# Transposing the inner activations of the feed-forward layers with VectorE blocks and a DRAM tile instead of TensorE

## The chip, the cores and the metric

One core of one Trainium2 chip runs the whole program. The metric is the device time of one execution in microseconds (us), the median of several executions.

## The reference, cut to what matters

Two layers, each a feed-forward layer, a mixer (attention, a state-space branch and a gating branch) and a second feed-forward layer, on 256 tokens of width 1024. The mixer is not touched by the change. The feed-forward layer is this:

```python
D_MODEL, SEQ, DEPTH, FFN_HIDDEN = 1024, 256, 2, 2816

def swiglu_ffn(x, w_gu, w_down):
    gate, up = jnp.split(x @ w_gu, 2, axis=-1)
    return (jax.nn.silu(gate) * up) @ w_down

def reference(...):
    h = x
    for i in range(DEPTH):
        f1 = swiglu_ffn(rms_norm(h, ffn1_pre_g[i]), ffn1_w_gu[i], ffn1_w_down[i])
        h = h + 0.5 * rms_norm(f1, ffn1_post_g[i])
        h = h + rms_norm(hybrid_mixer(...), mix_post_g[i])
        f2 = swiglu_ffn(rms_norm(h, ffn2_pre_g[i]), ffn2_w_gu[i], ffn2_w_down[i])
        h = h + 0.5 * rms_norm(f2, ffn2_post_g[i])
    return h
```

The product `silu(gate) * up` comes out with tokens on the partitions; the matmul with `w_down` needs it with the 2816 inner channels on the partitions. The step between the two, a transpose, is what is changed.

## The kernel before

**Tiling.** The 256 tokens are two tiles of 128 (t = 0, 1). Every weight matrix comes in blocks of 128 x 1024 float32 (512 KB); `load(i)` (L159) fetches block i into one of six `raw` tiles by a transfer issued from SyncE's queue. `split(i)` makes two float32r tiles of it, `whi` by a ScalarE cast (L179) and `wlo` by a VectorE subtraction (L180), in eleven buffers each, and then issues `load(i + 6)`. `unit` runs three matmuls for each 128 x 512 piece of a block and each token tile: high x high (L212), low x high (L213), high x low (L214). So a block feeds 4 matmuls of each of these lines, 12 in all.

**Feed-forward layer (`ffn`).** The 2816 inner channels are taken in six chunks, five of 512 and one of 256. For each chunk `gated` runs the gate and up matmuls into PSUM tiles `gu`, and `evac`, a task of its own, turns them into `silu` (ScalarE, L389) and `hh` (VectorE, L394). Then, in the kernel before, `evac` transposes `hh` on TensorE into a PSUM tile `htr`, 128 x 128 at a time (L401): eight transposes for a chunk of 512, four for the one of 256. ScalarE copies `htr` into `hTh` (L407) and VectorE subtracts to make `hTl` (L408). These two are the stationary operands of the down matmuls `dn`, which come after all six chunks, channel block by channel block.

**Order of the work.** The order of each engine is that in which the Python program emits its instructions (a manual schedule). After each unit of matmuls `pump` advances a nominal clock by 0.65 us for every three matmuls of 512 columns, steps every task whose waiting time has run out, and emits at most one split. A task's waiting times stand in the table `W`: `yield W["hh"]` in `evac` lets 5.2 us of this clock pass between `hh` and its transposes. The down matmuls call `finish(es[k // 4])` before they use a chunk, which steps that chunk's `evac` to its end if it is not there yet.

**SyncE's queue** issues its transfers in order, and each waits for what it needs before those behind it are issued. The weight loads are nearly all that is in it.

**Buffers.** `silu`, `hh` and other short-lived tiles of 128 x 512 share the six buffers of tag `b2`; `hTh` and `hTl` of a chunk of 512 are in `b4`. `htr` shares the three PSUM tiles of tag `tr` with the other transposes.

Of the kernel before, what the change touches and what calls it, by code (L numbers as in the profile page):

```python
# [9 lines left out]
F32 = mybir.dt.float32  # L10
# [3 lines left out]
ALU = mybir.AluOpType  # L14
AX = mybir.AxisListType

P = 128
L = 2
S = 256
NT = S // P  # L20
D = 1024
KD = D // P
FF = 2816
# [21 lines left out]
ACC, TR = 5, 3  # L45


W = {'gw': 6.5, 'tr': 0, 'parts': 0, 'sq': 1.3, 'lead': 3.9, 'sq2': 5.2, 'hh': 5.2, 'x0': 0.65, 'cv': 5.2, 'cs': 6.5, 'xs': 0, 'dt1': 2.6, 'dt2': 0, 'dt3': 5.2, 'cb': 2.6, 'w1': 1.3, 'w2': 5.2, 'ys': 3.9, 'qk': 3.9, 'vv': 0, 'qs': 0, 'ex': 0, 'p1': 10.4, 'p2': 0, 'p3': 3.9, 'ge': 0, 'ln': 10.4, 'sv': 0, 'yc': 9.1, 'mg': 3.9}


@with_exitstack
def trunk(ctx, tc, a):
    nc = tc.nc
    V, A, G, T = nc.vector, nc.scalar, nc.gpsimd, nc.tensor
# [2 lines left out]
    ring = ctx.enter_context(tc.tile_pool(name="ring", bufs=1))  # L57
    big = ctx.enter_context(tc.tile_pool(name="big", bufs=1))
    sm = ctx.enter_context(tc.tile_pool(name="sm", bufs=2))
    psum = ctx.enter_context(tc.tile_pool(name="psum", bufs=1, space=bass.MemoryType.PSUM))  # L60
    ctx.enter_context(tc.manual_schedule())

# [3 lines left out]
    def b2(name, shape=(P, 512), dt=F32):  # L66
        return big.tile(list(shape), dt, name=name, tag="b2", bufs=B2)
# [4 lines left out]
    def accs(name):  # L72

        slots = {}

        def dst(key, t):
            if (key, t) not in slots:
                slots[key, t] = acc(name)
            return slots[key, t]

        return slots, dst

    def tr(name):
        return psum.tile([P, 512], F32, name=name, tag="tr", bufs=TR)
# [8 lines left out]
    ident, tri, mask = (con[:, o:o + P] for o in (C_ID, C_TRI, C_MASK))  # L93
# [59 lines left out]
    raws, parts = {}, {}  # L153
# [38 lines left out]
    lead = [0]  # L192
# [56 lines left out]
    def chunk(key, kt=KD, n=512):  # L249
        per = 1024 // n  # L250
        return [[(b * per + j, j * n, n, key, b * per + j == 0, b * per + j == kt - 1) for j in range(per)]
                for b in range(kt // per)]


    def rsqrt(ss, name, scale, eps=EPS, coef=1.0):

        ss = list(ss)
        v = small(name + "v", 1)
        G.tensor_scalar(v, ss[0], scale / coef ** 2, eps / coef ** 2, op0=ALU.mult, op1=ALU.add)
        if len(ss) > 1:  # L260
            G.tensor_scalar(v, ss[1], scale / coef ** 2, v, op0=ALU.mult, op1=ALU.add)
        r = small(name, 1, bufs=4)
        G.tensor_tensor(r, v, nhalf, op=ALU.pow)
        return r

    def sumsq(src, name):
        ss = small(name, 1, bufs=4)
        junk = b2("junk", (P, src.shape[-1]), BF16)
        A.activation(junk, src, AF.Square, accum_out=ss)
        return ss  # L270

    def halves(ps, hi, lo):

        p3 = ps.rearrange("p (k t) -> p k t", k=4)
        A.copy(hi, p3)
        V.tensor_tensor(lo, p3, hi.bitcast(F32), op=ALU.subtract)

    def to_parts(src, hi, lo, gcol=None, scale=None, cut=((0, 4), (4, 8)), gap=W["parts"], made=None):

        for k0, k1 in cut:  # L280
            m = k1 - k0
            ps = tr("xtr")
            for k in range(k0, k1):
                T.transpose(ps[:, (k - k0) * P:(k - k0 + 1) * P], src[:, k * P:(k + 1) * P], ident)
            ps = ps[:, :m * P]
            if gcol is None:
                o_h, o_l = (x[:, k0:k1, :] for x in (hi, lo))
                p3 = ps.rearrange("p (k t) -> p k t", k=m)
                if scale is None:
                    A.copy(o_h, p3)  # L290
                    V.tensor_tensor(o_l, p3, o_h.bitcast(F32), op=ALU.subtract)
                else:
                    A.activation(o_h, p3, AF.Copy, scale=scale)
                    V.scalar_tensor_tensor(o_l, p3, scale, o_h.bitcast(F32), op0=ALU.mult, op1=ALU.subtract)
            else:
                o_h, o_l = (x[:, k0:k1, :] for x in (hi, lo))
                xg = b2("xg", (P, m, P))
                V.tensor_tensor(xg, ps.rearrange("p (k t) -> p k t", k=m),  # L298
                                gcol[:, k0:k1, None].to_broadcast([P, m, P]), op=ALU.mult)
                A.copy(o_h, xg)  # L300
                V.tensor_tensor(o_l, xg, o_h.bitcast(F32), op=ALU.subtract)  # L301
            if made is not None:
                made.update(range(k0, k1))
            yield gap

    class XT:
# [6 lines left out]
        def new(self, t):  # L313
            self.hi[t] = b4(f"{self.name}h{t}", (P, KD, P), F32R)
            self.lo[t] = b4(f"{self.name}l{t}", (P, KD, P), F32R)
            return self.hi[t], self.lo[t]
# [7 lines left out]
    def pre(t, x, r2, gcol, cut, made):  # L324

        yield from to_parts(h[t], *x.new(t), gcol=gcol, cut=cut, gap=2.0, made=made)
        yield W["sq"]
        r2[t] = rsqrt([sumsq(h[t], "s2")], "r2", 1.0 / D)

    class After:  # L330
# [13 lines left out]
        def run(self, t, grow, coef, x, r2, gcol, out):  # L344
# [25 lines left out]
            if out is None:  # L370
                yield W["lead"]
                yield from to_parts(h[t], *x.new(t), gcol=gcol)
            chains[0] -= 1
            if out is None:
                yield W["sq2"]
                r2[t] = rsqrt([sumsq(h[t], "s2")], "r2", 1.0 / D)


    def ffn(x, r2, nxt, head=HOLD):
        hT = {}  # L380
        es = {}

        def evac(c, w, gate, up):
            silu, hh = {}, {}
            for t in range(NT):
                while gate(t) is None:
                    yield 0
                silu[t] = b2("silu")
                A.activation(silu[t][:, :w], gate(t), AF.Silu, scale=r2[t])  # L389
            for t in range(NT):  # L390
                while up(t) is None:
                    yield 0
                hh[t] = b2("hh")
                V.scalar_tensor_tensor(hh[t][:, :w], up(t), r2[t], silu[t][:, :w], op0=ALU.mult, op1=ALU.mult)  # L394
            yield W["hh"]
            n = w // P
            pt = {}
            for t in range(NT):
                pt[t] = tr("htr")
                for j in range(n):  # L400
                    T.transpose(pt[t][:, j * P:(j + 1) * P], hh[t][:, j * P:(j + 1) * P], ident)  # L401
            new = b4 if n > 2 else b2
            hT[c] = (new("hTh", (P, NT, n, P), F32R), new("hTl", (P, NT, n, P), F32R))
            for t in range(NT):
                hi, lo = (z[:, t] for z in hT[c])
                p3 = pt[t][:, :w].rearrange("p (k t) -> p k t", k=n)
                A.copy(hi, p3)  # L407
                V.tensor_tensor(lo, p3, hi.bitcast(F32), op=ALU.subtract)  # L408

        def gated(c, w):  # L410
            slots, dst = accs("gu")
            full = set()

            def part(key, o):
                return lambda t: slots[key, t][:, o:o + w] if (key, t) in full else None

            halves_ = 2 if w == 512 else 1
            items = [b for key in range(halves_) for b in chunk(key)]
            es[c] = spawn(evac(c, w, part(0, 0), part(1, 0) if halves_ == 2 else part(0, w)))
            gemm(items, x.h, x.l, dst, head=head if c == 0 else 0, on_done=lambda key, t: full.add((key, t)))  # L420

        for c, w in enumerate(FCH):
            gated(c, w)
        items = [[(k, 512 * j, 512, j, k == 0, k == KF - 1) for j in range(2)] for k in range(KF)]

        def hx(i):
            def get(k, t):
                finish(es[k // 4])
                return hT[k // 4][i][:, t, k % 4, :]
            return get  # L430

        slots, dst = accs("dn")
        after = After(slots, nxt)
        gemm(items, hx(0), hx(1), dst, tail=HOLD, on_done=after, ends=nxt[-1] is not None)
        return after.tasks
# [14 lines left out]
    def spatial_weights(l):  # L450
        ws = b4("wsp", (P, 8, P))
        nc.sync.dma_start(ws, a["sgw"][l].rearrange("g j i -> j g i"))
        gb = row("sgu_ln_g", l), row("sgu_ln_b", l)
        yield W["gw"]
        V.tensor_tensor(ws, ws, tri[:, None, :].to_broadcast([P, 8, P]), op=ALU.mult)
# [579 lines left out]
    return v.reshape(lay, cols // n, k // (per * P), P, 1024)  # L1035


def _gated(w):
    parts = []
    c0 = 0  # L1040
    for n in FCH:
        halves = [w[:, :, half + c0:half + c0 + n] for half in (0, FF)]
        if 2 * n == 512:
            halves = [np.concatenate(halves, axis=2)]
        parts += [_chunks(m)[:, 0] for m in halves]
        c0 += n
    return np.ascontiguousarray(np.concatenate(parts, axis=1))
# [63 lines left out]
```

## Time and profile before

| | us |
|---|---|
| executions | 1506.69, 1508.36, 1509.73 |
| median | 1508.36 |
| the profiled execution, its own time | 1507.58 |
| span of its core, first to last instruction | 1505.8 |
| what lies around the span | 1.8 |

The profiled execution is 0.8 us below the median. The granted clock of TensorE is 0.997 of full speed over the span, its level of 2.4 GHz. In the profile PE is the matmuls of TensorE, PEld its weight loads, DVE is VectorE, ACT is ScalarE, POOL is GpSimd and SP is SyncE; a "q" behind the name means the queue of instructions that issue transfers. A matmul's duration there covers its way through the array, and the next one starts before it ends; the distance from start to start is the time that it takes of TensorE.

### The profile page before, as it was taken

How to read it: one execution, taken by the hardware profiler on the slowest of the kernel's cores; microseconds unless marked ns; L12 is line 12 of the kernel's file. 1: busy time of each engine (PE TensorE's matmuls, PEld its weight loads, DVE VectorE, ACT ScalarE, POOL GpSimd, SP SyncE). 2: the span in 40 equal slices, each digit the busy share in tenths (PEclk: the TensorE clock that was granted, in tenths of full speed). 3: DMA queues.
4: the chain of work that ended last, by engine and by line, in shares of the span. 5: the costliest groups of instructions: out<-in, count | busy, mean ns of one | idle time of the engine just before them, and what ended most of it. 6: DMA issues, size and time to landing. Idle time of an engine off the chain costs nothing.

```text
span 1505.8 us, 18575 instructions
## 1 busy us (share of the span) xinstructions
PE 1491.6 (99%) x7026; PEld 1236.4 (82%) x7026; DVE 932.2 (62%) x1112; ACT 783.2 (52%) x1079; POOL 55.8 (4%) x98
## 2 busy tenths in 40 slices
PE   9999999999999999999999999999999999999998
PEld 7888888878888888888888888888788888888886
DVE  6655477666566858555475554876665677675552
ACT  6544367655374537444364443866554644464441
POOL 0000020000000000000000000200000000000000
PEclk9999999999999999999999999999999999999999
DMA  8766646335556536666566664654364565476640
GB/s 292 269 191 196 185 169 193 116 124 182 159 179 212 180 138 224 205 182 201 153 225 185 184 205 140 210 168 141 116 190 142 195 197 168 153 254 192 183 154 28
DMA packets 77913, 270.27 MB, mean 179 GB/s; under 512 B 8960, under 2 KB 12160, under 8 KB 77824
## 3 DMA queue, kind: packets, MB, share of 16 engines
q1 hardware_dynamic: 77248, 268.76, 55.8%
q8 instruction: 55, 0.90, 0.2%
q10 hardware_dynamic: 576, 0.33, 0.1%
q14 instruction: 34, 0.28, 0.1%
HBM read 268.01 MB, written 1.05 MB: 179 GB/s over the span
## 4 chain that ended last, share of the span: by engine, by line
PE 94%; DVE 4%; ACT 1%; issue 1%; DMA 0%; POOL 0%; SPq 0%; DVEq 0%; ACTq 0%; POOLq 0%
PE gu L214 10%; PE gu L212 10%; PE gu L213 10%; PE dn L214 5%; PE dn L212 5%; PE dn L213 5%; PE br L214 3%; PE br L212 3%; PE br L213 3%; PE gate L212 2%; PE gate L214 2%; PE gate L213 2%; DVE wlo L180 2%; PE xbc L212 1%; PE xbc L213 1%; PE xbc L214 1%
## 5 line engine op out<-in xcount | busy, mean ns | idle before, releaser
L180 DVE TENSOR_TENSOR wlo<-raw,whi 128x1024 fp32r<-128x1024 f32 x495 | 601.5, 1234 | 385.8 <-ACT whi L179 384.6
L179 ACT CAST whi<-raw 128x1024 fp32r<-128x1024 f32 x495 | 513.5, 1051 | 406.0 <-PE gu L214 166.6
L212 PE MATMUL gu<-whi,xh 128*128 128x512 f32 x704 | 277.7, 394 | 1.8 <-ACT xh L300 1.4
L213 PE MATMUL gu<-wlo,xh 128*128 128x512 f32 x704 | 275.2, 391 | 0.0
L214 PE MATMUL gu<-whi,xl 128*128 128x512 f32 x704 | 274.8, 390 | 0.0
L212 PEld LDWEIGHTS gu<-whi,xh 128*128 128x128 f32 x704 | 132.6, 188 | 29.6 <-ACT xh L300 1.8
L214 PEld LDWEIGHTS gu<-whi,xl 128*128 128x128 f32 x704 | 132.6, 188 | 27.9 <-DVE xl L301 0.4
L213 PEld LDWEIGHTS gu<-wlo,xh 128*128 128x128 f32 x704 | 132.6, 188 | 27.7 <-DVE wlo L168 0.9
L212 PE MATMUL dn<-whi,hTh 128*128 128x512 f32 x352 | 137.9, 392 | 0.0
L214 PE MATMUL dn<-whi,hTl 128*128 128x512 f32 x352 | 137.1, 389 | 0.0
L213 PE MATMUL dn<-wlo,hTh 128*128 128x512 f32 x352 | 136.9, 389 | 0.0
L214 PEld LDWEIGHTS dn<-whi,hTl 128*128 128x128 f32 x352 | 66.1, 188 | 13.8
L212 PE MATMUL gate<-whi,xh 128*128 128x512 f32 x192 | 77.3, 403 | 0.0
L213 PEld LDWEIGHTS dn<-wlo,hTh 128*128 128x128 f32 x352 | 66.1, 188 | 13.4
L212 PEld LDWEIGHTS dn<-whi,hTh 128*128 128x128 f32 x352 | 66.1, 188 | 13.4
L214 PE MATMUL gate<-whi,xl 128*128 128x512 f32 x192 | 75.0, 390 | 0.0
L213 PE MATMUL gate<-wlo,xh 128*128 128x512 f32 x192 | 74.8, 390 | 0.0
L300 ACT CAST xh<-xg 128x512 fp32r<-128x512 f32 (+1 forms) x25 | 15.1, 603 | 62.0 <-DVE xg L298 62.0
L214 PEld LDWEIGHTS gate<-whi,xl 128*128 128x128 f32 x192 | 36.0, 188 | 7.8
L389 ACT ACTIVATE silu<-gu,r 128x512 f32<-128x512 f32 (+1 forms) x48 | 31.4, 654 | 19.9 <-PE gu L214 19.8
L213 PEld LDWEIGHTS gate<-wlo,xh 128*128 128x128 f32 x192 | 36.1, 188 | 6.6
L212 PEld LDWEIGHTS gate<-whi,xh 128*128 128x128 f32 x192 | 36.1, 188 | 6.5
(244 smaller groups left out, 2256.5 us busy)
## 6 DMA issues: line engine op xcount, KB each, us to landing
raw<-in_mix SPq DMA_DIRECT2D x232, 512.0 KB, 4.1
raw<-in_gu SPq DMA_DIRECT2D x175, 512.0 KB, 4.4
raw<-in_dn SPq DMA_DIRECT2D x88, 512.0 KB, 3.8
row_ffn_post_g<-in_ffn_post_g SPq DMA_DIRECT2D x4, 512.0 KB, 4.6
wsp<-in_sgw SPq DMA_DIRECT2D x2, 512.0 KB, 5.8
row_sgu_ln_g<-in_sgu_ln_g SPq DMA_DIRECT2D x2, 512.0 KB, 6.4
row_sgu_ln_b<-in_sgu_ln_b SPq DMA_DIRECT2D x2, 512.0 KB, 7.7
row_mix_post_g<-in_mix_post_g SPq DMA_DIRECT2D x2, 512.0 KB, 5.7
```

The lines of the kernel that those rows point to most:

```text
L179: A.copy(hi, w)
L180: V.tensor_tensor(lo, w, hi.bitcast(F32), op=ALU.subtract)
L212: T.matmul(o, xh(k, t), hi[:, off:off + n], start=first, stop=False)
L213: T.matmul(o, xh(k, t), lo[:, off:off + n], start=False, stop=False)
L214: T.matmul(o, xl(k, t), hi[:, off:off + n], start=False, stop=last)
L300: A.copy(o_h, xg)
L389: A.activation(silu[t][:, :w], gate(t), AF.Silu, scale=r2[t])
```

## The change

TensorE's transposes of `hh` go, and with them `htr`. In their place:

- `swap_out`, right behind `hh`: one VectorE transpose of the 128 x w tile, which transposes each 32 x 32 block in its place, into a tile `xt`, and one transfer (SyncE's queue) of `xt` to a tile in DRAM. Once for each token tile.
- after 6.5 us of the nominal clock `swap_in`: four transfers for each token tile (SyncE's queue) bring the DRAM tile back as `hr`. Each fills 32 partitions and reads runs of w/4 float32 (512 bytes for w = 512, 256 bytes for w = 256).
- after 6.5 us more `hTh` and `hTl` are made of `hr`, which is in SBUF, by the same two instructions as before; they read and write in pieces of 32 elements. Between the two token tiles 0.65 us pass.
- the columns of the gate and up weights are put in another order on the host (`_woven`), so that the blocks come out in the right places.

`silu`, `hh`, `xt` and `hr` share the six `b2` buffers. The DRAM tiles have eight buffers.

```diff
+    dram = ctx.enter_context(tc.tile_pool(name="dram", bufs=1, space=bass.MemoryType.DRAM))
...
+    def swap_out(src, w):
+        xt = b2("xt")
+        V.transpose(xt[:, :w], src[:, :w])
+        rd = dram.tile([P, w], F32, name=f"swap{w}", tag=f"swap{w}", bufs=8)
+        nc.sync.dma_start(rd, xt[:, :w])
+        return rd
+
+    def swap_in(dst, rd):
+
+        v = rd.rearrange("(a i) (c e) -> c i a e", a=4, c=4)
+        for c in range(4):
+            nc.sync.dma_start(dst[32 * c:32 * c + 32], v[c])
...
-            yield W["hh"]
             n = w // P
-            pt = {}
-            for t in range(NT):
-                pt[t] = tr("htr")
-                for j in range(n):
-                    T.transpose(pt[t][:, j * P:(j + 1) * P], hh[t][:, j * P:(j + 1) * P], ident)
+            rd = {t: swap_out(hh[t], w) for t in range(NT)}
+            yield W["out"]
+            hr = {}
+            for t in range(NT):
+                hr[t] = b2("hr")
+                swap_in(hr[t][:, :w].rearrange("p (a e) -> p a e", a=4), rd[t])
+            yield W["in"]
             new = b4 if n > 2 else b2
             hT[c] = (new("hTh", (P, NT, n, P), F32R), new("hTl", (P, NT, n, P), F32R))
             for t in range(NT):
-                hi, lo = (z[:, t] for z in hT[c])
-                p3 = pt[t][:, :w].rearrange("p (k t) -> p k t", k=n)
-                A.copy(hi, p3)
-                V.tensor_tensor(lo, p3, hi.bitcast(F32), op=ALU.subtract)
+                hi, lo = (z[:, t].rearrange("p k (a j) -> p a k j", a=4) for z in hT[c])
+                r4 = hr[t][:, :w].rearrange("p (a k j) -> p a k j", a=4, k=n)
+                A.copy(hi, r4)
+                V.tensor_tensor(lo, r4, hi.bitcast(F32), op=ALU.subtract)
+                yield 0.65
...
+def _woven(w, n):
+
+    v = w.reshape(*w.shape[:-1], -1, n // P, 4, 32)
+    return np.ascontiguousarray(v.swapaxes(-3, -2)).reshape(w.shape)
...
-        halves = [w[:, :, half + c0:half + c0 + n] for half in (0, FF)]
+        halves = [_woven(w[:, :, half + c0:half + c0 + n], n) for half in (0, FF)]
```

The table `W` gains `'out': 6.5, 'in': 6.5`.

## Rows read from the trace of the kernel before

**Rows 1.** The page: busy time of each engine with its share of the span, TensorE's granted clock in 40 slices, and the shares of the chain of work that ended last.

```profile
PE 1491.6 (99%) x7026; PEld 1236.4 (82%) x7026; DVE 932.2 (62%) x1112; ACT 783.2 (52%) x1079; POOL 55.8 (4%) x98
PEclk9999999999999999999999999999999999999999
PE 94%; DVE 4%; ACT 1%; issue 1%; DMA 0%; POOL 0%; SPq 0%; DVEq 0%; ACTq 0%; POOLq 0%
```

**Rows 2.** The waits of the whole span: who waited, for whom, us in total, times, the longest; then, of the view of the tile `raw`, all the waits of TensorE for a block that was made from it (us, times).

```profile
ACT whi L179 <- PE gu L214: 166.6, 117, 1.7
ACT whi L179 <- PE dn L214: 90.1, 55, 1.7
...
  PEld gu L212: 1.5, 2
  PEld gu L213: 1.4, 3
  PEld dtps L561: 0.7, 2
  PE gu L212: 0.3, 1
```

**Rows 3.** TensorE in order of time around the last eight transposes of a chunk of 512 and around the four of the chunk of 256 in the first layer. Columns: start, us from it to the end of the piece, engine, line, what it writes and reads, count.

```profile
131.64 0.39 PE L214 MATMUL gu<-whi,xl 128*128 128x512 f32 x1
131.87 1.03 PE L401 MATMUL htr<-con,hh 128*128 128x128 f32 x8
132.66 0.48 PE L212 MATMUL gu<-whi,xh 128*128 128x512 f32 x1
...
134.12 0.39 PE L212 MATMUL gu<-whi,xh 128*128 128x512 f32 x1
...
142.28 0.39 PE L212 MATMUL dn<-whi,hTh 128*128 128x512 f32 x1
...
143.41 0.39 PE L214 MATMUL dn<-whi,hTl 128*128 128x512 f32 x1
143.64 0.60 PE L401 MATMUL htr<-con,hh 128*128 128x128 f32 x4
144.00 0.48 PE L212 MATMUL dn<-whi,hTh 128*128 128x512 f32 x1
...
145.24 0.39 PE L214 MATMUL dn<-whi,hTl 128*128 128x512 f32 x1
```

**Rows 4.** The instructions that touch the tile `htr`: the transposes with the least, median and greatest duration in ns, and their busy time over the whole span by engine (PE, PEld, DVE, ACT), overlaps counted once.

```profile
L401 PE MATMUL htr<-con,hh x176: 270/272/273, 41.2 to 1446.0; 128*128 128x128 f32 x176
...
0.00:1505.80 1505.80, 23.07 (x176) 20.59 (x176) 28.76 (x48) 24.09 (x48) 1.00 0.56 179
```

**Rows 5.** The tile `wlo` from the start to five moments: busy time and count of the instructions on PE (the matmuls of L213 that read it), PEld, and DVE (the blocks made, the first of them in two halves).

```profile
0.00:40.00 40.00, 16.80 (x40) 7.95 (x41) 20.36 (x18) 1.00 0.85 299
0.00:109.00 109.00, 54.81 (x138) 26.23 (x138) 53.23 (x45) 1.00 0.76 252
0.00:594.00 594.00, 298.31 (x763) 144.11 (x763) 240.55 (x199) 1.00 0.57 185
0.00:780.00 780.00, 401.01 (x1026) 193.52 (x1026) 321.44 (x266) 1.00 0.58 187
0.00:1338.00 1338.00, 684.84 (x1754) 330.86 (x1755) 542.04 (x448) 1.00 0.57 182
```

**Rows 6.** Two stretches of one chunk of 512 each, in the first and second feed-forward layer: busy us of PE, PEld, DVE, ACT and POOL with the count of instructions, then TensorE's granted clock, the share of the transfer engines, GB/s.

```profile
109.00:131.60 22.60, 22.60 (x105) 18.84 (x104) 12.42 (x12) 10.72 (x13) 0.00 (x0) 1.00 0.66 185
599.00:621.60 22.60, 22.60 (x105) 18.83 (x104) 12.77 (x13) 10.98 (x13) 0.00 (x0) 1.00 0.75 243
```

**Rows 7.** Groups of VectorE and ScalarE instructions by shape: busy us, mean ns of one, idle time before them.

```profile
L842 DVE TENSOR_SCALAR gate<-gate,rs 128x512 f32<-128x512 f32 x8 | 3.5, 480 | 0.0
L859 DVE TENSOR_TENSOR merged<-merged,gate 128x512 f32<-128x512 f32 x16 | 11.1, 692 | 0.6
L811 DVE SCALAR_TENSOR_TENSOR vg<-vg,mv,row_sgu_ln_g 128x1024 f32<-128x1024 f32 x4 | 5.1, 1284 | 0.1
L408 DVE TENSOR_TENSOR hTl<-htr,hTh 128x512 fp32r<-128x512 f32 x40 | 25.8, 686 | 1.8
L407 ACT CAST hTh<-htr 128x512 fp32r<-128x512 f32 x40 | 21.5, 589 | 13.9 <-PE htr L401 13.9
L300 ACT CAST xh<-xg 128x512 fp32r<-128x512 f32 x23 | 14.3, 620 | 59.1 <-DVE xg L298 59.1
```

**Rows 8.** Transfers. A group by what it loads, with KB each and the median us from issue to landing; the load `wsp`, whose runs in DRAM are 512 bytes, with its time to landing (least, median, greatest); a weight load's time in SyncE's queue (ns) and its time to landing; and the transfer engines in the stretch from 590 to 600 us, in which the first chunk of the second feed-forward layer ends.

```profile
wsp<-in_sgw SPq DMA_DIRECT2D x2, 512.0 KB, 5.8
raw<-in_gu SPq DMA_DIRECT2D x175, 512.0 KB, 4.4
...
DMA to landing us min/median/max: 5.6/5.8/5.9
...
L159 SPq DMA_DIRECT2D raw<-in_gu x175: 327/328/772, 2.6 to 1393.4; - x175
...
DMA to landing us min/median/max: 3.3/4.2/9.1
...
DMA packets 1052, 3.83 MB, mean 383 GB/s; under 512 B 116, under 2 KB 116, under 8 KB 1052
```

More of the change, by code (lines that the diff above doesn't have):

```diff
@@ L45 @@
 ACC, TR = 5, 3
-W = {'gw': 6.5, 'tr': 0, 'parts': 0, 'sq': 1.3, 'lead': 3.9, 'sq2': 5.2, 'hh': 5.2, 'x0': 0.65, 'cv': 5.2, 'cs': 6.5, 'xs': 0, 'dt1': 2.6, 'dt2': 0, 'dt3': 5.2, 'cb': 2.6, 'w1': 1.3, 'w2': 5.2, 'ys': 3.9, 'qk': 3.9, 'vv': 0, 'qs': 0, 'ex': 0, 'p1': 10.4, 'p2': 0, 'p3': 3.9, 'ge': 0, 'ln': 10.4, 'sv': 0, 'yc': 9.1, 'mg': 3.9}
+W = {'gw': 6.5, 'tr': 0, 'parts': 0, 'sq': 1.3, 'lead': 3.9, 'sq2': 5.2, 'hh': 5.2, 'x0': 0.65, 'cv': 5.2, 'cs': 6.5, 'xs': 0, 'dt1': 2.6, 'dt2': 0, 'dt3': 5.2, 'cb': 2.6, 'w1': 1.3, 'w2': 5.2, 'ys': 3.9, 'qk': 3.9, 'vv': 0, 'qs': 0, 'ex': 0, 'p1': 10.4, 'p2': 0, 'p3': 3.9, 'ge': 0, 'ln': 10.4, 'sv': 0, 'yc': 9.1, 'mg': 3.9, 'out': 6.5, 'in': 6.5}
 @with_exitstack
```

## The prediction

> **What bounds the kernel now.** I read the page first: TensorE is busy for 99% of the span at a granted clock of nine tenths or more in every slice, and the chain that ended last runs 94% over PE, 4% over DVE [rows 1]. A busy PE need not be one without slack, since a matmul's row overlaps the next, so I looked next for waits. TensorE waits for a block of weights only eight times, 3.9 us in all, while ScalarE waits for TensorE in 172 places before it may write the next `whi`, 257 us in all [rows 2]: the eleven block buffers are full and the helpers are ahead. How far ahead is counted from the tile `wlo`: up to 109 us, 44 blocks were made and 138 / 4 = 34.5 used, so 9.5 blocks lie ready; at 594 us 198 - 190.8 = 7; at 780 us 265 - 256.5 = 8.5; at 1338 us 447 - 438.5 = 8.5; at 40 us, just ahead of the first transposes, 17 - 10.3 = 6.7 [rows 5]. Of TensorE's own pace the timeline tells: 36 starts from 134.12 to 142.28 us, 0.227 us each [rows 3]. A block of 12 matmuls is 2.72 us, and seven blocks are 19 us of cover. So here the end is set by what TensorE is given to do, and an instruction taken off it in this stage shortens the kernel by its time from start to start.
>
> **What is removed.** The row of a transpose says 0.272 us, and 176 of them would be 47.9 us; with overlaps counted once they cover 23.1 us [rows 4]. Neither is what they cost. From the last matmul ahead of eight transposes to the seventh start behind them pass 134.12 - 131.64 = 2.48 us, where seven starts take 7 x 0.227 = 1.59: eight transposes cost 0.89 us, 0.79 of it before the next matmul starts and 0.10 in the slower starts behind it. The four of the last chunk cost 145.24 - 143.41 - 6 x 0.227 = 0.47 us [rows 3]. There are 4 feed-forward layers with five groups of eight and one of four: 20 x 0.89 + 4 x 0.47 = 19.7 us. The lower bound counts only the gap before the next matmul, 20 x 0.79 + 4 x (144.00 - 143.41 - 0.227) = 17.3 us; the upper one is the 23.1 us covered. I take 19.7, as it is the distance of starts that the chain is made of.
>
> **What VectorE gets.** One transpose of 128 x 512 for each token tile; the trace has none. From below it is bounded by the cheapest one-source instruction of this shape, 0.48 us, from above by one of twice the width, 1.28 us; I take the 0.69 of an ordinary instruction of this shape [rows 7], as it also has one element in and one out for each lane and column. That adds 2 x 0.69 = 1.4 us to a chunk (1.0 to 2.6) in which VectorE works 12.4 to 12.8 of 22.6 us [rows 6]: about 14, at most 15.4, of the 21.7 us that are left of the chunk without the 0.89. Behind the transposes in VectorE's order stands the `wlo` of a block that TensorE needs seven to ten blocks later; 1.4 us against 19 of cover cost nothing. With the cover gone they would cost TensorE 20 x 1.4 + 4 x 0.7 = 31 us.
>
> The Trainium skill, "VectorE: DVE Perf Modes", section "The three transpose paths", gives 311 ns for a VectorE transpose of 128 x 128 in 16 bits; by that figure four in float32 would be an estimate of up to 1.2 us a tile, and no run here shows it yet. It lies inside the bounds above.
>
> **What moves from PSUM to SBUF.** The cast that makes `hTh` now reads SBUF: 620 instead of 589 ns for such a cast; the subtraction 692 instead of 686 [rows 7]. Both are off the path, 24 x 2 x 0.04 = 2 us in all. That they walk in runs of 32 elements no row prices; at twice their time a chunk has 2.6 us more on each engine, still under the idle 9.8 us of VectorE and 11.6 of ScalarE [rows 6].
>
> **What SyncE and the transfers get.** Per chunk two transfers out and eight in: 10 x 0.33 = 3.3 us of issuing beside the 8 x 0.33 of the weight loads [rows 8], in 22 us. The first `swap_out` waits for VectorE's transpose, the first `swap_in` for the landing in DRAM; behind them in the queue stand weight loads, six blocks (16 us) ahead of their split. The bytes are 1 MB a chunk; at the 383 GB/s that the transfer engines reached when they were full [rows 8] that is 2.7 us, on engines busy for 66 to 75% of such a chunk [rows 6], so 78 to 87% afterwards. That counts short runs like long ones; from the other side, a load of the same 512 KB with runs of 512 bytes, `wsp`, took 5.8 us to land against the 4.4 of a weight load [rows 8]. So the two `hr` land some 6 us after their issue, and `evac` asks for them 6.5 us of its clock later, 6.8 in time (0.227 x 3 for 0.65). If they are late, ScalarE stands still before `hTh` with the `whi` of later blocks behind it, and the cover pays. Nobody needs `hTh` soon: the last chunks' are asked for behind 32 units of the down matmuls, 32 x 6 x 0.227 = 44 us later. Cost: nothing; bound, one late landing of the longest kind (9.1 us [rows 8]) in each of 24 chunks, 24 x 2.3 = 55 us of ScalarE, which its idle 11 us a chunk absorb.
>
> The rule that speaks against this change stands in the Trainium skill, "DMA: Bandwidth & Descriptors", section "Rules for kernel authors": do not transpose in a transfer by a rearranged access pattern, it is 19 times slower than the hardware's own transposing transfer. Here only whole runs of 128 floats are moved about, and the row of `wsp`, a load with such runs, shows 1.3 times a weight load, not 19 times; the rule is weighed below as a rival.
>
> **The sum.** On TensorE -19.7 us; everything else is added beside it. The profiled execution: 1507.58 - 19.7 = 1487.9 us; it lies 0.8 below the median, so the median goes to 1508.4 - 19.7 = 1488.7.
>
> **The rivals.**
> - *Part is given back.* In the first chunk of a layer the blocks are still being caught up: around 594 us the transfer engines run at 383 GB/s, all they gave anywhere, with 7 blocks ready [rows 5, 8]. The new megabyte puts the loads back by 2.7 us and VectorE by 1.4 more; if that reached TensorE in the first chunk of each layer, 4 x 4.1 = 16 us at worst, about 8 on a middle course: 1497. Against it: 7 blocks are 19 us.
> - *No gain.* TensorE's pace is set by the supply of blocks, so the freed time turns into waiting: 1508. For it speaks only that VectorE is on 4% of the chain [rows 1]; against it the 3.9 us of waits and the seven to ten blocks ready [rows 2, 5].
> - *Slower: `hr` lands late.* ScalarE stands before `hTh`, all splits behind it. It decides from a landing at 6.8 + 11.6 = 18.4 us after issue on, in every chunk, plus what the cover of 19 us in six chunks gives (3.2): above 21.6 us a chunk loses. At 25 us: 24 x 3.4 = 82 us lost, 1570. The rows nearest to it say 5.8 and 9.1 [rows 8].
> - *Slower: strided reads at a 19th of the rate.* If the rows in DRAM read back 19 times as slowly as a weight load's 4.4 us for 512 KB, a chunk would need 84 us of transfers instead of its 22: about 20 x 62 + 4 x 31 = 1360 us more, near 2870. The page of that rule is named above; the `wsp` row is against it.
>
> **How the numbers follow.** Full gain 0.80 (its own range 1485.3 to 1491.1, from the bounds 23.1 and 17.3); part given back 0.10; no gain 0.04; late landing 0.04; strided reads 0.02. The range takes in the first and most of the second: 1485 to 1496. What a measurement of this kernel can tell from no change is about 0.2%, 3 us: faster 0.80 + 0.10 = 0.90, same 0.04, slower 0.06. The predicted time is that of the full gain, 1488.7.
>
> **What would show it.** In the profile of the changed kernel: no matmul of L401, 6850 instead of 7026 matmuls, PE's chain at the same 0.227 us from start to start through the whole of a chunk, which lasts 21.8 instead of 22.65 us; VectorE's transposes near 0.7 us, 48 of them; waits of PE for `whi` or `wlo` still a few us. It would be wrong if PE showed gaps within the gate and up matmuls (a given-back gain, then the waits name DVE or a transfer), if ScalarE's wait before `hTh` for the transfer of `hr` were over 10 us a chunk, or if the pace of matmuls itself got slower beside the new transfers.

## The result, and the profile after

The changed kernel takes 1487.53 us (median; 1486.74 to 1488.53) against 1508.37 of the kernel before: a ratio of 0.9863, 95% interval 0.9846 to 0.9880, or 20.8 us less. The prediction was 1488.7, 19.7 us less. The profiled executions differ by the same: spans of 1505.8 and 1486.2 us, 19.6 apart.

The page of the changed kernel, the lines that answer to [rows 1]; the lines of the program are moved, so that the matmuls L212 to L214 are now L213 to L215, and L179, L180 are L180, L181:

```profile
PE 1472.1 (99%) x6850; PEld 1218.8 (82%) x6850; DVE 955.2 (64%) x1160; ACT 782.6 (53%) x1079; POOL 55.6 (4%) x98
PE 94%; DVE 4%; ACT 1%; issue 1%; POOL 0%; DMA 0%; DVEq 0%; ACTq 0%; POOLq 0%
```

176 matmuls fewer, PE's busy time 19.5 us shorter, and the same chain. The first down matmul of the first layer in the kernel before, then the same place in the changed kernel:

```profile
136.84 0.39 PE L212 MATMUL dn<-whi,hTh 128*128 128x512 f32 x1
```

```profile
131.94 0.39 PE L215 MATMUL gu<-whi,xl 128*128 128x512 f32 x1
132.16 0.39 PE L213 MATMUL dn<-whi,hTh 128*128 128x512 f32 x1
```

The down part starts 4.7 us earlier. Five groups of eight transposes lay ahead of it, and 5 x 0.89 is 4.5. What came in their place, on VectorE and ScalarE (groups by shape: busy us, mean ns | idle before, and for whom), and the transfers of the way back (count, KB each, median us to landing):

```profile
L277 DVE STREAM_TRANSPOSE xt<-hh 128x512 f32<-128x512 f32 x40 | 25.9, 687 | 0.0
L425 DVE TENSOR_TENSOR hTl<-hr,hTh 128x512 fp32r<-128x512 f32 x40 | 27.4, 686 | 8.3 <-ACT hTh L424 8.2
L424 ACT CAST hTh<-hr 128x512 fp32r<-128x512 f32 x40 | 24.7, 617 | 13.1 <-DMA hr<-swap 12.6 <-issue 0.2
...
hr<-swap SPq DMA_DIRECT2D x160, 64.0 KB, 4.9
```

Two chunks of 512, as [rows 6] showed them before (busy us of PE, PEld, DVE, ACT, POOL; granted clock, share of the transfer engines, GB/s), and the waits that matter: ScalarE for `hr`, and SyncE's queue at the way back:

```profile
109.00:131.00 22.00, 22.00 (x98) 18.21 (x98) 13.66 (x15) 10.72 (x12) 0.00 (x0) 1.00 0.80 240
596.00:618.00 22.00, 22.00 (x98) 18.21 (x97) 14.20 (x15) 10.98 (x13) 0.00 (x0) 1.00 0.91 308
...
ACT hTh L424 <- DMA hr<-swap: 19.4, 12, 4.5
...
SPq L286 <- DMA raw<-in_gu: 28.3, 21, 2.4
...
140.78 7.47 SPq L286 DMA_DIRECT2D hr<-swap  x8
```

TensorE is without a gap in both. VectorE has 1.2 to 1.4 us more, the transfer engines are at 80 and 91%, and ScalarE stood before `hTh` in 12 of 48 cases, 4.5 us at the longest. The eight transfers of a chunk's way back are in SyncE's queue for 5 to 7.5 us (the row is the short chunk of the first layer), not for the 2.6 that eight times 0.33 make: by the profile some wait for transfers issued before them.

### The profile page after: what moved, and what is told of

It reads as the page before. It is cut to its first block, busy times and chain, and to the rows that moved or that the text cites. A ratio compares the mean times of both kernels' runs of the same rounds, so it can differ in the third digit from the quotient of the medians.

```text
span 1486.2 us, 18786 instructions
## 1 busy us (share of the span) xinstructions
PE 1472.1 (99%) x6850; PEld 1218.8 (82%) x6850; DVE 955.2 (64%) x1160; ACT 782.6 (53%) x1079; POOL 55.6 (4%) x98
## 4 chain that ended last, share of the span: by engine, by line
PE 94%; DVE 4%; ACT 1%; issue 1%; POOL 0%; DMA 0%; DVEq 0%; ACTq 0%; POOLq 0%
PE gu L213 11%; PE gu L215 11%; PE gu L214 11%; PE dn L213 5%; PE dn L215 5%; PE dn L214 5%; PE br L213 3%; PE br L215 3%; PE br L214 3%; PE gate L215 2%; PE gate L213 2%; PE gate L214 2%; DVE wlo L181 2%; PE xbc L215 1%; PE xbc L213 1%; PE xbc L214 1%
## 5 line engine op out<-in xcount | busy, mean ns | idle before, releaser
L181 DVE TENSOR_TENSOR wlo<-raw,whi 128x1024 fp32r<-128x1024 f32 x495 | 600.2, 1232 | 331.1 <-ACT whi L180 319.8
L180 ACT CAST whi<-raw 128x1024 fp32r<-128x1024 f32 x495 | 512.8, 1051 | 380.9 <-PE gu L215 131.8
L213 PE MATMUL gu<-whi,xh 128*128 128x512 f32 x704 | 276.0, 392 | 1.4 <-ACT xh L316 1.4
L214 PE MATMUL gu<-wlo,xh 128*128 128x512 f32 x704 | 274.9, 391 | 0.0
L215 PE MATMUL gu<-whi,xl 128*128 128x512 f32 x704 | 274.8, 390 | 0.0
L213 PEld LDWEIGHTS gu<-whi,xh 128*128 128x128 f32 x704 | 132.7, 188 | 29.8 <-ACT xh L316 1.8
L215 PEld LDWEIGHTS gu<-whi,xl 128*128 128x128 f32 x704 | 132.6, 188 | 28.0 <-DVE xl L317 0.4
L214 PEld LDWEIGHTS gu<-wlo,xh 128*128 128x128 f32 x704 | 132.5, 188 | 27.9 <-DVE wlo L169 0.9
L213 PE MATMUL dn<-whi,hTh 128*128 128x512 f32 x352 | 137.5, 391 | 0.0
L215 PE MATMUL dn<-whi,hTl 128*128 128x512 f32 x352 | 137.0, 389 | 0.0
L214 PE MATMUL dn<-wlo,hTh 128*128 128x512 f32 x352 | 136.9, 389 | 0.0
L215 PEld LDWEIGHTS dn<-whi,hTl 128*128 128x128 f32 x352 | 66.1, 188 | 13.8
L213 PE MATMUL gate<-whi,xh 128*128 128x512 f32 x192 | 77.3, 403 | 0.0
L214 PEld LDWEIGHTS dn<-wlo,hTh 128*128 128x128 f32 x352 | 66.1, 188 | 13.5
L213 PEld LDWEIGHTS dn<-whi,hTh 128*128 128x128 f32 x352 | 66.1, 188 | 13.4
L215 PE MATMUL gate<-whi,xl 128*128 128x512 f32 x192 | 75.0, 391 | 0.0
L214 PE MATMUL gate<-wlo,xh 128*128 128x512 f32 x192 | 74.8, 390 | 0.0
L215 PEld LDWEIGHTS gate<-whi,xl 128*128 128x128 f32 x192 | 36.0, 188 | 7.7
L405 ACT ACTIVATE silu<-gu,r 128x512 f32<-128x512 f32 (+1 forms) x48 | 31.3, 654 | 19.8 <-PE gu L215 16.2
L214 PEld LDWEIGHTS gate<-wlo,xh 128*128 128x128 f32 x192 | 36.2, 188 | 6.6
L213 PEld LDWEIGHTS gate<-whi,xh 128*128 128x128 f32 x192 | 36.1, 188 | 6.6
```

The costliest lines, as they stand in the source:

```text
L180: A.copy(hi, w)
L181: V.tensor_tensor(lo, w, hi.bitcast(F32), op=ALU.subtract)
L213: T.matmul(o, xh(k, t), hi[:, off:off + n], start=first, stop=False)
L214: T.matmul(o, xh(k, t), lo[:, off:off + n], start=False, stop=False)
L215: T.matmul(o, xl(k, t), hi[:, off:off + n], start=False, stop=last)
```

## The experiments

Each edit is to the changed kernel. Ratios are to the kernel before, run on the same chip, with their 95% interval.

**No transposition at all.**

```diff
-            rd = {t: swap_out(hh[t], w) for t in range(NT)}
-            yield W["out"]
...
-            yield W["in"]
+            yield W["hh"]
+            hr = hh
```

> Leaves the transposition of the inner activations out altogether: hTh and hTl are made straight from hh, so the down matmuls multiply other numbers of the same shapes. Neither TensorE's transposes nor VectorE's, and no transfer through DRAM. Theory (the gain is TensorE's time for the transposes, and all that was added lies beside it): the same time as the changed kernel, 1487.5 us, within 1.5. Rival (the added work costs something that the gain hides): clearly under the changed kernel, by 3 us or more.

Measured: 1487.04 us, 0.9860 (0.9847 to 0.9873). The changed kernel's 0.9863 is within this: VectorE's transposes and 23 MB of transfers there and back cost nothing that can be measured, and the intervals are some 2 us wide to either side.

**TensorE's transposes put back beside the new path.**

```diff
             rd = {t: swap_out(hh[t], w) for t in range(NT)}
-            yield W["out"]
+            yield W["hh"]
+            for t in range(NT):
+                pt = tr("htr")
+                for j in range(n):
+                    T.transpose(pt[:, j * P:(j + 1) * P], hh[t][:, j * P:(j + 1) * P], ident)
+            yield W["out"] - W["hh"]
```

> The changed kernel with TensorE's transposes of hh put back at their old place, 5.2 us of the nominal clock behind hh, into a PSUM tile that nobody reads; hTh and hTl still come by VectorE and DRAM. Theory: 1487.5 + 19.7 = 1507.2 us, level with the kernel before. Rival (part of the gain is of another source, as the later making of hTh or the freed PSUM tiles): 1503 or less. Rival (the added work costs something): 1511 or more.

Measured: 1506.93 us, 0.9998 (0.9989 to 1.0006), level with the kernel before. So the gain is the time of the 176 transposes on TensorE: 1506.9 - 1487.5 = 19.4 us by the medians, 20.4 by the two ratios. Any other part of it is too small for these intervals.

**No waiting times.**

```diff
-'out': 6.5, 'in': 6.5}
+'out': 0, 'in': 0}
```

> The changed kernel with both waiting times at nothing ('out': 0, 'in': 0): the way back from DRAM is asked for as soon as the way out is issued, and ScalarE's cast to hTh stands in its queue at once. Theory (the blocks made ahead are cover enough): ScalarE waits some 8 to 12 us for hr in each of the 24 chunks, about 250 us in all against 19 in the changed kernel, SyncE waits for the landing in DRAM with weight loads behind it, and the time stays at 1487.5 within 2. Rival (the waiting times are what hides the transfers): 24 x 10 us less what ScalarE has idle, from 1495 up to 1600.

Measured: 1515.98 us, 1.0053 (1.0041 to 1.0065). The theory fell: 28 us lost. ScalarE's wait was as expected, but not what it held up. The waits of this kernel, and then ScalarE, VectorE and TensorE in order of time at the end of the first layer's gate and up matmuls, with the granted clock behind the stop and later:

```profile
ACT hTh L424 <- DMA hr<-swap: 251.7, 37, 11.7
...
PE dn L213 <- DVE hh L410: 20.5, 4, 6.5
...
134.82 0.62 ACT L424 CAST hTh<-hr 128x512 fp32r<-128x512 f32 x1 [10.61 <-DMA hr<-swap]
...
139.09 0.83 ACT L405 ACTIVATE silu<-gu,r 128x256 f32<-128x256 f32 x2
...
140.55 0.87 DVE L410 SCALAR_TENSOR_TENSOR hh<-gu,r,silu 128x256 f32<-128x256 f32 x2
...
134.14 0.39 PE L215 MATMUL dn<-whi,hTl 128*128 128x512 f32 x1
141.08 0.80 PE L213 MATMUL dn<-whi,hTh 128*128 128x512 f32 x1 [6.55 <-DVE hh L410]
141.67 0.63 PE L214 MATMUL dn<-wlo,hTh 128*128 128x512 f32 x1
142.10 0.63 PE L215 MATMUL dn<-whi,hTl 128*128 128x512 f32 x1
...
141.00:146.00 5.00, 4.92 (x15) 3.98 (x16) 2.20 (x5) 0.00 (x0) 0.00 (x0) 0.67 0.95 301
146.00:150.00 4.00, 4.00 (x20) 3.30 (x19) 0.00 (x0) 0.00 (x0) 0.00 (x0) 1.00 0.73 252
```

ScalarE stands 10.6 us before the cast of the last full chunk. Behind it in its order is the `silu` of the short chunk, whose matmuls end 10.9 us after the full one's; VectorE's `hh` waits for that `silu`, and the down matmul at 141.08 takes the PSUM tile that this `hh` reads. TensorE waits there once in each of the four layers, 20.5 us in all, and behind this stop the granted clock is 0.67 for 5 us, that is, partly at the lower level. ScalarE's other waits, over 200 us, cost nothing, as the next run shows.

**The waiting times only where the short chunk follows.**

```diff
-            yield W["out"]
+            yield W["out"] if c == 4 else 0
...
-            yield W["in"]
+            yield W["in"] if c == 4 else 0
```

> Both waiting times at nothing, as in the run without lead, except in the chunk ahead of the short one (c = 4), which keeps 6.5 and 6.5. New theory (what a late hr holds up are not the splits but silu and hh of the next chunk, whose PSUM tiles TensorE needs; only the short chunk follows so soon that its silu stands behind the cast of hr): ScalarE still waits some 200 us for hr in all, TensorE has none of the four stops at the start of the down matmuls, 1487.5 us within 2. Old theory of the splits as what is held up: the wait is nearly as long as without lead, so about 1512.

Measured: 1487.93 us, 0.9871 (0.9857 to 0.9886). The whole gain is back, with ScalarE's wait for `hr` still at 213.5 us; of TensorE's waits the longest in all is again the mixer's:

```profile
ACT hTh L424 <- DMA hr<-swap: 213.5, 29, 14.0
...
PE ctr L513 <- DVE ssw L682: 3.1, 2, 1.6
```

Four places of 24 needed the waiting times.

**Short runs: weights not reordered, 128 bytes a run, sixteen transfers for a token tile.**

```diff
-        v = rd.rearrange("(a i) (c e) -> c i a e", a=4, c=4)
-        for c in range(4):
-            nc.sync.dma_start(dst[32 * c:32 * c + 32], v[c])
+        v = rd.rearrange("(a i) (k c j) -> c a i k j", a=4, c=4, j=32)
+        d = dst.rearrange("p a (k j) -> p a k j", j=32)
+        for c in range(4):
+            for b in range(4):
+                nc.sync.dma_start(d[32 * c:32 * c + 32, b], v[c, b])
```

> The changed kernel without the new order of the gate and up weights' columns: the way back reads runs of 32 floats (128 bytes) instead of 128 (512 bytes), in sixteen transfers for each token tile instead of four. Theory (bytes and packets count, and short runs are not much slower): 4 times the packets of the way back, about 3 us more of transfers a chunk and 24 more issues in SyncE's queue, 10 us a chunk; hr lands later, ScalarE waits more, the time stays at 1488 to 1492. Rival (short runs are ruinous): 84 us a chunk, over 2500 us; a rate of a quarter would give some 8 us more a chunk and still be covered.

Measured: 1713.13 us, 1.1363 (1.1349 to 1.1378). Neither number. A stretch as long as a chunk of before, and one of TensorE's waits:

```profile
109.00:131.00 22.00, 22.00 (x87) 17.94 (x87) 10.23 (x11) 6.45 (x8) 0.00 (x0) 0.88 0.55 167
...
PE dn L213 <- ACT whi L180: 29.0, 5, 8.3
```

The transfer engines are not full, at 55%. TensorE waits 136 us for `hh`, and here also 29 us for `whi`: the cover of blocks made ahead runs out in the down parts. To tell the count of transfers from the length of their runs, the next run has the count alone.

**Long runs, but sixteen transfers for a token tile.**

```diff
         for c in range(4):
-            nc.sync.dma_start(dst[32 * c:32 * c + 32], v[c])
+            for b in range(4):
+                nc.sync.dma_start(dst[32 * c:32 * c + 32, b], v[c, :, b])
```

> The changed kernel with its runs of 512 bytes, but in sixteen transfers for each token tile instead of four, as many as in the run with short runs. Theory A (the count of transfers is the cost: SyncE issues them one by one at 0.4 to 0.6 us and weight loads stand behind them): near the 1713 us of the short runs, 1650 or more. Theory B (short runs are the cost, in the issue or in the engines): 1488 to 1510.

Measured: 1602.27 us, 1.0637 (1.0615 to 1.0658), between the two theories. The count alone costs 115 us, the short runs on top 111. The issue in SyncE's queue with its ns (least, median, greatest), with short runs; with long runs the way back of one chunk in that queue, ScalarE at the same time, and two waits of TensorE's weight loads:

```profile
L288 SPq DMA_DIRECT2D hr<-swap x768: 538/597/1718, 46.7 to 1682.3; - x192
```

```profile
132.06 16.16 SPq L287 DMA_DIRECT2D hr<-swap  x32
...
142.22 0.62 ACT L425 CAST hTh<-hr 128x512 fp32r<-128x512 f32 x1 [9.73 <-DMA hr<-swap]
...
149.51 0.62 ACT L425 CAST hTh<-hr 128x512 fp32r<-128x512 f32 x1 [5.72 <-DMA hr<-swap]
...
PEld dn L213 <- DVE hh L411: 41.9, 8, 6.9
PEld gu L213 <- DVE hh L411: 40.3, 9, 6.4
```

32 transfers are 16.2 us of SyncE's queue with long runs (a median of 0.42 each, the rest waits) and at 0.60 each 19 us with short ones, of a chunk of 21.8 that also needs its weight loads issued. The second `hr` lands some 17 us after the first issue, ScalarE stands before `hTh` twice, 15 us in this chunk, and `silu` and `hh` are late in ordinary chunks too. The profiled executions are 112 us apart: 78 of it is more idle time of PE (91.8 us against 14.1), the other 34 is more busy time for the same matmuls (1506.6 against 1472.1), at a mean granted clock of 0.974.

**Each VectorE transpose nine times.**

```diff
-        V.transpose(xt[:, :w], src[:, :w])
+        for _ in range(9):
+            V.transpose(xt[:, :w], src[:, :w])
```

> The changed kernel with each VectorE transpose made nine times: 16 more of 0.67 us in a chunk of 512, 10.8 us on VectorE, which then has 24.4 us of work in a chunk of 21.8. Theory of the splits as cover: 2.6 us too much in each of five chunks and less in the short one, 13 to 15 us a layer against 19 us of cover, so 1488 to 1492. Theory of silu and hh: hr comes 10.8 us later and hh of the short chunk stands behind the transposes, TensorE stops at the start of the down matmuls in each layer, 4 times 5 to 10 us: 1510 to 1530.

Measured: 1664.39 us, 1.1041 (1.1021 to 1.1060), over both numbers, on the side of `silu` and `hh`. Two of TensorE's waits, one of ScalarE's, and the two `silu` of one chunk:

```profile
PE dn L213 <- DVE hh L411: 89.7, 8, 15.8
...
PE gu L213 <- DVE hh L411: 49.1, 9, 7.4
...
ACT silu L406 <- DVE xt L278: 89.9, 20, 5.7
...
78.76 0.69 ACT L406 ACTIVATE silu<-gu,r 128x512 f32<-128x512 f32 x1 [5.25 <-DVE xt L278]
80.80 0.69 ACT L406 ACTIVATE silu<-gu,r 128x512 f32<-128x512 f32 x1 [1.35 <-DMA swap<-xt]
```

139 us are for `hh`, in the full chunks too; I had counted stops at the short one alone. `silu` was late in its turn by a thing I had not thought of: the `b2` buffer that it is to write is one that the transposes of the chunk before still use. The first `silu` starts when the nine transposes of one token tile are through, the second has to wait for the transfer of an `xt` on top. None of the longer waits is for a block of weights. The rest is slower matmuls: the mean granted clock was 0.952, and PE's busy time for the same matmuls grew by 33 us, from 1472.1 to 1505.5.

**Twice the bytes.**

```diff
+        for r in range(2):
+            more = dram.tile([P, w], F32, name=f"more{w}", tag=f"more{w}", bufs=16)
+            nc.sync.dma_start(more, xt[:, :w])
         return rd
```

> The changed kernel with two more transfers of every xt to DRAM tiles that nobody reads: 1 MB more a chunk of 512, which doubles the bytes of the new path, and four more issues in SyncE's queue. Theory (while the transfers fit in a chunk and hr comes before the silu of the short chunk is held up, they cost nothing): 2.7 us more on transfer engines that are busy for 80 to 91% of a chunk, just full; hr lands some 3 to 5 us later, ScalarE's wait for it goes from 19 to 50 or 100 us, 1488 to 1492. Rival (no room left): stops of TensorE at the start of the down matmuls, 1495 or more.

Measured: 1486.67 us, 0.9857 (0.9842 to 0.9872). Two chunks, the waits for `hr` in all (us, times), and the longest of a full chunk:

```profile
109.00:131.00 22.00, 22.00 (x99) 18.22 (x98) 14.40 (x17) 10.61 (x13) 0.00 (x0) 1.00 0.92 307
596.00:618.00 22.00, 22.00 (x99) 18.22 (x98) 13.48 (x15) 10.77 (x13) 0.00 (x0) 1.00 0.95 322
...
  DMA hr<-swap: 103.4, 26
...
79.00 0.62 ACT L427 CAST hTh<-hr 128x512 fp32r<-128x512 f32 x1 [7.95 <-DMA hr<-swap]
```

Engines at 92 and 95%, 103 us of waits on ScalarE, 4 us each and up to 8 in a full chunk, and no loss: the changed kernel has room for this.

**The transfers alone transpose, 4 bytes a run.**

```diff
-        V.transpose(xt[:, :w], src[:, :w])
...
+            for k in range(n):
+                nc.sync.dma_start(d[:, k, :], rd[:, k * P:(k + 1) * P].rearrange("t p -> p t"))
```

> The transfers alone make the transposition: hh goes to DRAM as it is, and the way back reads one float32 at a time, 65536 runs of 4 bytes for a token tile; no VectorE transpose, and no new order of the weights' columns. It is the case of the rival of strided reads. If a chunk then needs 84 us for its way back, 22 chunks' worth cost 22 x 84 us of transfers beside the weight loads: about 2700 to 3000 us. If runs that short cost no more than the 512-byte ones (the rule does not hold here): 1490 to 1700.

Measured: 3544.88 us (one execution). This is above both ranges. The issue of the way back in SyncE's queue:

```profile
L287 SPq DMA_DIRECT2D hr<-swap x176: 377/13484/15932, 45.8 to 3495.5; - x176
```

Eight of them make a chunk of 512: 8 x 13.5 = 108 us, where I had guessed 84. So the rival of the strided reads was a real one for runs of one element, and none for runs of 128. The 108 us are 25 times the 4.4 in which a weight load of as many bytes lands [rows 8]. The Trainium skill, "DMA: Bandwidth & Descriptors", section "Rules for kernel authors", puts such a transfer at 19 times the hardware's transposing one. No run here has that one, so its ratio is neither shown nor refuted; that the pattern is ruinous is.

**The same for q and k in the mixer.** The transposes of q and k (64) made by VectorE and DRAM as well, k landing in the operand itself, q with one ScalarE copy; the weights' columns of both are reordered.

```diff
+            rd = [swap_out(toks[t], 512) for t in range(NT)]
+            yield W["out"]
+            for t in range(NT):
+                swap_in(o[:, t].rearrange("p a k j -> p a (k j)"), rd[t])
...
-            yield from transposed(toks, lambda t: o[:, :, t * P:(t + 1) * P], "a")
```

> The changed kernel, with the transposes of q and k in the mixer made in the same way: 64 of TensorE's transposes less, 16 VectorE transposes and 160 transfers more; k lands from DRAM straight in the operand of the score matmuls, without a ScalarE copy, q is copied once by ScalarE. Theory: 8 groups of eight at 0.89 us, 7.1 us less, and up to 3 us more as TensorE's waits at the old transposes go (two of 1.6 us behind ssw): 1477.5 to 1480.4. Rival (the queues of the mixer have no room, or k is late): 1487 or more.

Measured: 1491.51 us, 0.9896 (0.9882 to 0.9911): 4 us slower than the changed kernel. TensorE's waits in the changed kernel, and in this one, with VectorE at the place, and the stretch of the branch with the lowest granted clock in each:

```profile
PE ctr L513 <- DVE ssw L682: 3.2, 2, 1.6
PE seg L680 <- DVE xg L314: 1.6, 2, 0.8
...
312.00:318.00 6.00, 6.00 (x21) 4.78 (x20) 4.26 (x5) 3.78 (x9) 0.00 (x0) 0.72 0.28 85
```

```profile
PE yd L711 <- DVE ssw L688: 5.9, 3, 2.7
PE seg L680 <- DVE xg L314: 3.2, 2, 1.6
PE yd L711 <- DVE xs L671: 2.9, 2, 1.5
...
307.10 1.29 DVE L277 STREAM_TRANSPOSE xt<-qtok 128x512 f32<-128x512 f32 x2
308.32 0.65 DVE L314 TENSOR_TENSOR xg<-xtr,par 128x512 f32<-128x512 f32 x1
...
318.00:330.00 12.00, 9.34 (x34) 7.17 (x34) 8.80 (x12) 5.70 (x12) 0.00 (x0) 0.72 0.47 129
```

Here TensorE waits for VectorE's state-space branch, in order. The waits grow from 4.8 to 12.0 us, as much as the 7.1 us of transposes, and the stretch with a clock of 0.72 is 12 us long instead of 6. So PE's busy time falls by only 3.4 us (1472.1 to 1468.7), while its idle time grows by 7.8. For the wait for `xg` the rows show VectorE's transposes right ahead of it; that they also make `ssw` and `xs` late was not shown by itself.

**Later emission of the branch.**

```diff
-'w2': 5.2,
+'w2': 7.8,
```

> The kernel with q and k transposed by VectorE and DRAM as well, and the waiting time w2 of the state-space branch raised from 5.2 to 7.8 us, so that TensorE's instructions that wait for ssw come later in its order. Theory (the 7.1 us of transposes went into TensorE's waits for ssw, as VectorE's transposes stand ahead of ssw): these waits shrink from some 15 us to under 6, 1478 to 1484. Rival (the branch itself is then late, and what follows waits for it): 1490 or more.

This is the version with q and k and a longer `w2`. Measured: 1505.31 us, 0.9983 (0.9974 to 0.9993). The rival was right. The wait for `ssw` that the edit was aimed at shrank from 5.9 to 3.9 us, but the branch's end, which nothing covers, comes later, and a new wait is the longest:

```profile
PE xtr L300 <- DVE y L722: 13.3, 2, 6.6
```

**q alone.**

```diff
+            if which == "q":
+                s = b4("qs", (P, NT, 4, 4, 32))
+                rd = [swap_out(toks[t], 512) for t in range(NT)]
...
+                return
             yield W["qk"]
```

> The changed kernel with the transposes of q alone, not of k, made by VectorE and DRAM as well (q is ready ahead of most of the state-space branch; 32 of TensorE's transposes less, 8 VectorE transposes and 80 transfers more). Theory (what cost the version with q and k its gain are VectorE's transposes ahead of ssw and TensorE's clock after each wait, and q comes before them): 4 groups at 0.89 us less, 1483.5 to 1485.5. Rival (the mixer's VectorE has no room at q's place either): 1487 or more.

Measured: 1488.49 us, 0.9877 (0.9860 to 0.9894), the same as the changed kernel. Again TensorE's waits for the branch take it:

```profile
PE ctr L513 <- DVE xg L314: 3.8, 2, 1.9
PE ctr L513 <- DVE ssw L682: 3.2, 2, 1.6
PE seg L680 <- DVE xg L314: 2.7, 2, 1.4
```

9.7 us instead of 4.8, for 3.6 us of transposes less. None of the three versions of the mixer beats the changed kernel.

## Why the prediction was right, point by point

- **What bounds the kernel** and **what is removed**: right. Both runs on the transposes alone say so: put back beside the new path they bring the time of before, left out without a substitute they give the time of after. The distance from start to start gave 19.7 us; the medians say 20.8 and the spans 19.6, which is within the spread of the executions. The row's 0.272 us each would have given 47.9.
- **VectorE's transpose**: taken as 0.69 us, measured 0.687. The busy time of a chunk came out at 13.7 to 14.2, as the sum said.
- **The casts from SBUF**: 617 and 686 ns against 620 and 692. The runs of 32 elements cost nothing. The bound for them was added up wrongly: 2.6 us is both engines together, 1.2 on ScalarE and 1.4 on VectorE.
- **The transfers**: shares of 80 to 91% against 78 to 87. SyncE's issue was mis-sized: 5 to 7.5 us for the way back instead of 2.6, as a transfer of it takes 0.42 us and some wait. The landing was said to be some 6 us after the issue, `evac` asking after 6.8. A transfer landed 4.9 us after its own issue, but the last of eight is issued 5 to 7 us after the first, so that ScalarE did wait, 19.4 us in all. And 383 GB/s was not all that the transfer engines gave: from 780 to 790 us of the kernel before it was 397.
- **The cover**: this step was wrong, and it was luck that the time did not show it. The prediction said that a late `hr` holds up the `whi` of blocks that are seven to ten ahead, with 19 us of cover. What is behind it in ScalarE's order and needed first is `silu`, and through `hh` the PSUM tiles that TensorE takes next. In a full chunk the cast is asked for 13.6 us after its `hh` and the next `hh` is due at 21.8, so by estimate 8 us of lateness are free. The runs bear this out: waits of up to 8 us cost nothing (twice the bytes), 9.7 and 5.7 us in one chunk belong to a loss of 115 us (sixteen transfers). The blocks made ahead gave out in earnest only with the short runs, with 29 us for `whi` beside 136 for `hh`. Ahead of the short chunk the two waiting times, 13.0 of the nominal clock against the 10.4 that its matmuls take, are what puts the cast behind its `silu`; without them the kernel is slower than before. The prediction gave no reason of this kind for them.
- **The rival of a late landing**: right in kind, wrong in size. It was to decide from 21.6 us after the issue. With sixteen transfers the second `hr` lands some 17 us after the first issue, and that kernel is at 1602. What kept it away is that four transfers a tile, in 512-byte runs, land in time; the reordered weights and the waiting times are what makes the change work. The rival of the strided reads has a slip in its sum: 1360 us more than the predicted 1488.7 are near 2850, not 2870.
- **No gain** and **part given back** did not come: TensorE's waits for blocks did not grow: six, 2.8 us in all, against eight and 3.9. In the changed kernel, too, the transfer engines are full around the end of a first chunk, and TensorE has no gap there; up to 594 us 201 blocks were made and 770 / 4 = 192.5 used, so 8.5 lie ready where it was 7 [rows 5, 6]. The first row has the columns of [rows 6], the second those of [rows 5]:

```profile
590.00:600.00 10.00, 10.00 (x46) 8.29 (x45) 8.00 (x9) 6.84 (x8) 0.00 (x0) 1.00 1.02 392
...
0.00:594.00 594.00, 301.47 (x770) 145.51 (x770) 243.05 (x202) 1.00 0.60 198
```

## What to carry to other kernels

Work moved off a bounding engine is worth its time from start to start there, if the engine does not already wait at that place: the same move was worth some 20 us in the feed-forward layers and nothing in the mixer, where TensorE waits for VectorE. Price the substitute by what stands behind its waiting instruction in that engine's order, down to the first thing that the bound engine needs, not by the deepest buffer. And count transfers as well as bytes: the same bytes in four times as many cost 115 us through the queue that issues them.

## What was not expected of the hardware

- After a stop of some 7 us TensorE's granted clock was 0.67 over the next 5 us and 1.00 behind that; starts were 0.43 us apart instead of 0.227 (141.67 to 142.10 us in the run without waiting times). So a stop costs more than its length.
- The time of a transfer in SyncE's queue was the longer, the shorter its runs: a median of 0.33 us for a weight load, 0.42 for 64 KB or 16 KB in 512-byte runs, 0.60 for 16 KB in 128-byte runs, 13.5 for 64 KB in 4-byte runs. The length of the runs is not all of it: a load that repeats one row of 4 KB for every partition (`row_ffn_post_g`) took 0.43.
